# Weight sets moved to places of 1,056 columns, in a hybrid encoder layer on one Trainium2 core

## The chip, the core and the metric

The kernel runs on one core of one Trainium2 chip. A core has a matrix engine (TensorE; PE in the profile, its weight loads PEld), a vector engine (DVE), a scalar engine (ACT), GpSimd (POOL) and SyncE (SP), which here only issues transfers. They share an on-chip memory of 128 partitions. A TensorE instruction pair is a weight load of a 128x128 block and a matmul that streams up to 512 columns of a second operand, the moving one, through it. The metric is device microseconds of one execution. Three runs of the kernel before gave 1048.36, 1048.68 and 1045.71 us, the median is 1048.36.

## What is computed

One encoder layer over 512 positions of width 1024, in float32, with batch and depth of one. Modulation, norms, rotary embedding, a windowed and a differential attention and two gated feed-forward blocks:

```
mod = silu(c) @ w_mod + b_mod                      # nine vectors: shift, scale, gate three times
h = modulate(rmsnorm(x), sh1, sc1)
x = x + 0.5 * g1 * (silu(h @ w_gate1) * (h @ w_up1)) @ w_ffn1_out
h = modulate(rmsnorm(x), sh2, sc2)
qa, ka, va, qb, kb, vb, ga, gb = split(h @ w_in)
ya = window_gqa_sink(rope(norm(qa)), rope(norm(ka)), va) @ w_branch_a
yb = (rmsnorm(diff_attention(rope(norm(qb)), rope(norm(kb)), vb)) * 0.8) @ w_branch_b
x = x + g2 * ((sigmoid(ga) * ya + sigmoid(gb) * yb) @ w_out)
h = modulate(rmsnorm(x), sh3, sc3)
x = x + 0.5 * g3 * (silu(h @ w_gate3) * (h @ w_up3)) @ w_ffn2_out
```

The feed-forward width is 2816, so the two blocks hold most of the products.

## The kernel before

Every float32 operand of a product is split into a rounded part ("high") and the rest ("low"), and a product of blocks is three matmuls: high weights by high data, high by low, low by high. Line 173 (`mm3`) writes these three at lines 174 to 176. Line 437 (`two`) does the same for two blocks of 256 columns at lines 443 to 445; it serves the `Unit` class, which computes the feed-forward products by a seven-product scheme on quarter matrices. Lines 1125 to 1127 and 1144 to 1146 are projections in which the roles are changed: the weights' high and low parts are the moving operand and the hidden state is the stationary one. Line 681 is the first product of the kernel.

**Where weights lie.** A weight set of up to 1024 columns comes by DMA into a `raw` buffer, ACT rounds it into a set of the tile `high`, DVE writes the rest into the same columns of the tile `low` (`split_from`, line 189), or, in `load_main` (line 1059) and for three of the first sets, ACT and an accumulating DMA write the low part. Each of the two tiles has five places (HILO, line 98), taken in turn by `high_low` (line 197) unless a place is held. Places are 1024 columns apart, and a set may start some columns further on: the argument `aside`. The starts are ASIDE = 16 columns in every `Unit` (line 491), in the two later sets of line 923, in `project_pairs` (1136), in one gate (1165), in some sets of the last products of the first block (854), of a branch (1601) and of the mixing product (1663); FAR = 64 columns in the other sets of `Out1` (854); 8 or 56 in two steps from one rule to the next; 0 for the rest (first products, `project`, most gates, the other branch, six of the eight mixing sets). A set of 1024 columns that starts 16 columns aside ends in the first 16 columns of the next place. Dependencies are tracked by address, so there a write waits for the readers of the neighbour.

**Addresses.** Tiles are laid out in each partition in the order of their first use in the code, each rounded up to 32 bytes. Counting from the start of the pool at byte 4224: `high` begins at 22848 and `low` at 43584, both 64 bytes past a multiple of 256; the moving tiles `b8` (twelve of 8192 bytes from 68672) and `ka` also begin 64 past one, and the tiles `u4` (six of 4096 bytes from 167072) 160 past one. All slices of `b8` and `u4` that are used as operands start at multiples of 512 bytes in their tile. Blocks of weights are 128 columns, 512 bytes, apart. So the place of a weight block against its moving operand, taken modulo 256 bytes, is settled by the start of its set: 16 columns are 64 bytes, and 64 columns are 256. The text below calls (address of the weights minus address of the moving operand) modulo 256 bytes the **distance** of a matmul. It is 64 for the sets at 16 columns with `b8` as the moving operand, 0 for those at 0 and 64 columns, and 192 in the projection of line 1144, where the set (at 128) moves and `b8` (at 64) is stationary.

**What orders the work.** Most of the kernel is under a manual order for TensorE, DVE and ACT or for the queues: `run_items` (line 533) asks for each weight set some products ahead of its use and splits it some products ahead (ASK and MAKE, lines 459 and 460); a planner (`Line`, line 47) orders the attention.

Of the kernel before, what the change touches and what calls it, by code (L numbers as in the profile page):

```python
# [11 lines left out]
F32 = mybir.dt.float32  # L12
# [6 lines left out]
P = 128  # L19
# [77 lines left out]

RAW, HILO, F2 = 4, 5, 8

ASIDE = 16  # L100

FAR = 64


STEP, STEP_1 = 8, 56
BRANCH_ASIDES = (STEP, ASIDE, ASIDE, ASIDE), (ASIDE, ASIDE, 0, 0)
MIX_ASIDES = 0, 0, 0, 0, 0, 0, ASIDE, ASIDE

CHUNKS = (range(0, 6), range(6, 12), range(12, 16), range(16, 22))
PLAIN, LAST_1 = 3, 4  # L110
# [24 lines left out]
def layer(ctx: ExitStack, tc: tile.TileContext, a: dict):  # L135
# [58 lines left out]
    split = []  # L194
    turn, holders = [0], {}

    def high_low(n=1024, aside=0, holder=None):
        while turn[0] % HILO in holders:
            turn[0] += 1
        i = turn[0] % HILO  # L200
        turn[0] += 1
        if holder:
            holders[i] = holder
        i = i * 1024 + aside
        return tuple(t[:, i : i + n] for t in parts)

    def let_go(holder):
        for i in [i for i in holders if holders[i] == holder]:
            del holders[i]

    def load_split(src, n=1024, spare=False, aside=0):
        raw = sbuf("raw", [P, 1024], F32, RAW)
        if spare:
            hi, lo = (u4().rearrange("p a b -> p (a b)") for _ in range(2))
        else:
            hi, lo = high_low(aside=aside)
        nc.sync.dma_start(raw[:, 0:n], src)
        split_from(hi[:, 0:n], lo[:, 0:n], raw[:, 0:n])
        return hi, lo
# [4 lines left out]
    half = keep([P, 8], "half")  # L224
    V.memset(half, -0.5)
    S.activation(small(8), half, AF.Silu)
    ones = keep([P, P], "ones")
    V.memset(ones, 1.0)
    ident = keep([P, P], "ident")
    make_identity(nc, ident)  # L230

    par = keep([P, NPAR], "par")
    x = [xt() for _ in range(NC)]
    parts, modv = [], []
    for nm, n in (("high", 6), ("low", 9)):
        parts.append(keep([P, HILO * 1024 + ASIDE], nm, F32R))
        modv += [keep([P, NC], f"mod{v}") for v in range(len(modv), n)]
    sub8, lam_s, nlam = (keep([P, n], nm) for nm, n in (("sub8", 1), ("lam_s", 2), ("nlam", 1)))

    def mod_load(v, c, w=None):  # L240
        if w is None:
# [42 lines left out]
    class Norm:  # L284
# [41 lines left out]
        def sums(self, sq, r, first, last):  # L326
            if first:
                self.st[r.start] = bank("op" if r.start else "tp")
            for t in range(r.start // P, r.stop // P):
                i = 2 * (t - r.start // P)  # L330
                PE.matmul(
                    self.st[r.start][:, i : i + 2], sq[:, t * P : (t + 1) * P], ones[:, 0:2],
                    start=first and i == 0, stop=last and (t + 1) * P == r.stop, skip_group_check=True,
                )

# [111 lines left out]
    class Unit:  # L447
# [33 lines left out]
        def prepare(self, q):  # L481

            if q in self.ready:
                return
            self.ask(q)
            n = self.depth * 2 * P
            if q in self.apart:
                both = b8().rearrange("p a b -> p (a b)")
                hi, lo = both[:, 0:n], both[:, 1024 : 1024 + n]
            else:  # L490
                hi, lo = high_low(n, ASIDE, (self, q))
            t = self.at[q]
# [108 lines left out]

    cact = [sbuf("ka", [P, D], F32, 1)]
    hh, hl = new_h()
    ccol = keep([P, 3 * NC], "ccol")[:, 0:NC]
    nc.scalar.dma_start(ccol, a["c"])
    tc.keep_in_program_order(nc.scalar.dma_start(par, a["par"]))
    for c in range(NC):
# [2 lines left out]
    with tc.manual_schedule(engines=BOUND | {mybir.EngineType.SP, mybir.EngineType.Pool}):  # L610
# [14 lines left out]
                start=j == 0, stop=j == 3, skip_group_check=True,  # L625
            )
        warm(3)
        w1, pos = {}, []

        def first_loads(k):  # L630
            scale = mod_load(SC1, k)
            if k == 0:
                pos.append(keep([P, NT], "pos", I32))
            shift = mod_load(SH1, k) if k == 0 else None
            raw = sbuf("raw", [P, 1024], F32, RAW)
            nc.sync.dma_start(raw, a["w1s"][k])
            w1[k] = [scale, shift or mod_load(SH1, k), raw]
# [137 lines left out]
    pos = pos[0]  # L775
# [57 lines left out]
    class Out1:  # L833
# [14 lines left out]
        def by_halves(self, m):  # L848
            return self.final and m >= NC - LAST_1

        def prepare(self, m):
            if m not in self.ready:
                self.ask(m)
                aside = FAR if not self.by_halves(m) else STEP_1 if m == NC - LAST_1 else ASIDE
                if self.final and m == 0:
                    while turn[0] % HILO != 1:
                        turn[0] += 1
                t = self.ready[m] = high_low(self.depth * P, aside, (self, m))
                with tc.issue_after(copied[0]):
                    split_from(*t, self.at[m])  # L860

# [51 lines left out]
    with tc.manual_schedule(engines={mybir.EngineType.SP, mybir.EngineType.Pool}):  # L913
# [4 lines left out]
        for q in range(4, 2 * PLAIN):  # L918

            w, sums_from = loaded1, split[1]  # L920
            if q < 5:
                with tc.issue_after(split[0]), tc.issue_after(split[1]):
                    loaded1 = [load_split(a["w1i"][1, k], aside=ASIDE) for k in range(2)]
# [12 lines left out]
            if q == 4:  # L936
                units1[PLAIN].prepare("s1")
            side1(1.0)
# [44 lines left out]
    V.tensor_scalar(sub8, par[:, SUBLN : SUBLN + 1], 1.0 - LAM_INIT, None, ALU.mult)  # L983

    NF = HD // 2
    posf = keep([P, NT], "posf")
    V.tensor_copy(posf, pos)
    tb = u4(F32)
    tb = [tb[:, i, :] for i in range(2)]
# [66 lines left out]

    hh, hl = new_h()

    def load_main(src, aside=0):

        raw = sbuf("raw", [P, 1024], F32, RAW)
        nc.sync.dma_start(raw, src)
        hi, lo = high_low(aside=aside)
# [67 lines left out]
    def project_pairs(srcs, then):  # L1131

        n = 2 * P
        out = [bank("acc") for _ in range(2)]
        for u, src in enumerate(srcs):
            wh, wl = load_main(src, ASIDE)
            for t in range(NT):
                ht = slice(t * P, (t + 1) * P)
                po = out[t // 2][:, t % 2 * n : (t % 2 + 1) * n]
                for i in range(4):  # L1140
                    k = 4 * u + i
                    w = slice(i * n, (i + 1) * n)
                    first, last = k == 0 and t % 2 == 0, k == NC - 1 and t % 2 == 1
                    PE.matmul(po, hh[k][:, ht], wh[:, w], start=first, stop=False, skip_group_check=True)
                    PE.matmul(po, hh[k][:, ht], wl[:, w], start=False, stop=False, skip_group_check=True)
# [14 lines left out]
    def gates(more=lambda: True):  # L1160
        while gate_next[0] < 16 and more():
            j = gate_next[0]
            gate_next[0] += 1

            wh, wl = load_main(a["w_gate"][j], ASIDE * (j == EARLY_A))
# [77 lines left out]

    kb_h, kb_l, vb_h, vb_l, qb_h, qb_l = (b8() for _ in range(6))
    rqb = keep([P, NT, 8], "rqb")
    nrqb = keep([P, NT, 8], "nrqb")
    ob_h, ob_l = b8(), b8()
    done, turns = {"a": 0, "b": 0}, {"a": 0, "b": 0, "o": 0, "w": (0, 0), "q": 0, "t": 0}

# [143 lines left out]
    def tables_a():  # L1393
# [1 line left out]
        nc.sync.dma_start(late, table_scr)  # L1395
        table["qa"], table["ka"] = (four(late)[i : i + 2] for i in (0, 2))
        ka = sbuf("ka", [P, 2, T], F32R, 1)
        wa.update(k=(ka[:, 0, :], ka[:, 1, :]), rq=keep([P, NT, 8], "rqa"))

    def two_blocks(raw, nh, tabs, i, rs, scale8):  # L1400

# [193 lines left out]
            turns["w"] = (b, g * nk + kc + 1)  # L1595


    def branch(w, j0, o_h, o_l, then, load, r=FULL[0], asides=(0, 0, 0, 0)):
        for u in range(4):
            with tc.issue_after(banded_last[0]):  # L1600
                wh, wl = load(w[u], aside=asides[u])
            for i in range(2):
                j = 2 * u + i
                g = f2()[:, r]
# [8 lines left out]
    def main():  # L1613
# [30 lines left out]

        for i, r in enumerate(HALVES):
            line.drain(lambda: done["a"] >= 2 * i + 2)
            yield from branch(a["w_ya"], 0, *wa["o"], then_b, load_split, r, BRANCH_ASIDES[i])

    mix = []
    line.run(main())  # L1650
# [9 lines left out]
    nc.sync.dma_start(cact[0], c_scr.partition_broadcast(P))  # L1660
    mod_begin(G3)
    for m in range(NC):
        w = load_split(a["w_mix"][m], aside=MIX_ASIDES[m])

        def products(po, r, w=w):
            wh, wl = w
# [367 lines left out]
```

## Time and profile before

| | |
|---|---|
| median of three runs | 1048.36 us |
| the profiled execution | 1044.11 us, span from first to last instruction 1042.3 us |
| granted TensorE clock | 0.999 of full |
| TensorE busy | 1034.8 us, 99% of the span, 7348 matmuls |
| weight loads busy | 953.2 us, 91% |
| DVE, ACT, POOL busy | 785.5 us, 575.6 us, 165.7 us |
| moved | 220.92 MB, mean 212 GB/s |
| chain of work that ended last | TensorE 93%, DVE 3%, ACT 3% |

Busy time of TensorE says little by itself here: matmuls overlap each other, and the profile models their ends. The time from the start of one to the start of the next is what adds up to the span. It can be read from the timeline, which lists each matmul with its start: the starts of the first matmul of a stretch and of the first one behind it, divided by the number between them. The mean duration of a group is the modelled one, and it rises with the same stalls.

### The profile page before, as it was taken

To read this page: it belongs to the slowest core of one execution; us is meant where nothing else is said; L and a number is where in the kernel's file an instruction comes from. 1 tells how busy PE (TensorE), PEld (TensorE's weight loads), DVE (VectorE), ACT (ScalarE), POOL (GpSimd) and SP (SyncE) were. 2 spreads that over 40 slices of the span, in tenths; PEclk is the share of its full clock that TensorE was granted. 3 is DMA by queue.
4 is the path that set the end of the run, shared out by engine and by line. 5 is a ranking of instruction groups with operands and counts; after the bars stand their busy time and mean duration, and the time that the engine had idled before them with its cause. 6 is when DMAs were issued, how large, how long until landed. Compare 5 with 4: busy or idle time off the path is not lost.

```text
span 1042.3 us, 18751 instructions
## 1 busy us (share of the span) xinstructions
PE 1034.8 (99%) x7348; PEld 953.2 (91%) x7348; DVE 785.5 (75%) x1436; ACT 575.6 (55%) x948; POOL 165.7 (16%) x190
## 2 busy tenths in 40 slices
PE   9999999999999999999999999999999999999998
PEld 6889899899998998899888888989999999999998
DVE  6886667567796679859772588976899777877867
ACT  6664335234454442667785855525867556655553
POOL 1101110110110100543333101001111111112110
PEclk9999999999999999999999999999999999999999
DMA  9977786966984459796646834974498998989874
GB/s 366 346 218 187 242 235 198 275 173 180 259 207 150 149 203 410 232 261 140 179 97 184 242 124 158 366 229 112 98 238 190 244 226 206 231 216 220 208 150 127
DMA packets 68793, 220.92 MB, mean 212 GB/s; under 512 B 8288, under 2 KB 10976, under 8 KB 68704
## 3 DMA queue, kind: packets, MB, share of 16 engines
q1 hardware_dynamic: 46224, 146.52, 38.7%
q0 software_dynamic: 19344, 68.70, 35.1%
q10 hardware_dynamic: 3136, 4.51, 1.2%
q8 instruction: 57, 0.93, 0.3%
q14 instruction: 32, 0.26, 0.1%
HBM read 209.46 MB, written 10.23 MB: 211 GB/s over the span
## 4 chain that ended last, share of the span: by engine, by line
PE 93%; DVE 3%; ACT 3%; issue 0%; DMA 0%; POOL 0%; DVEq 0%; ACTq 0%; POOLq 0%
PE acc L443 7%; PE acc L444 7%; PE acc L445 7%; PE sc L443 6%; PE sc L445 6%; PE sc L444 6%; PE sc L174 5%; PE sc L175 5%; PE sc L176 5%; PE acc L174 4%; PE acc L176 4%; PE acc L175 4%; PE acc L1125 2%; PE acc L1126 2%; PE acc L1127 2%; PE tp L1203 1%
## 5 line engine op out<-in xcount | busy, mean ns | idle before, releaser
L190 ACT CAST high<-raw 128x1024 fp32r<-128x1024 f32 (+2 forms) x160 | 155.9, 985 | 149.8 <-PE sc L175 37.7
L190 DVE TENSOR_TENSOR low<-raw,high 128x1024 fp32r<-128x1024 f32 (+2 forms) x160 | 181.3, 1141 | 49.4 <-ACT high L190 48.5
L443 PE MATMUL acc<-b,high 128*128 128x256 f32 x508 | 140.9, 277 | 0.0
L444 PE MATMUL acc<-b,high 128*128 128x256 f32 x508 | 140.7, 277 | 0.1
L445 PE MATMUL acc<-b,low 128*128 128x256 f32 x508 | 140.6, 277 | 0.0
L445 PE MATMUL sc<-b,low 128*128 128x256 f32 x500 | 138.5, 277 | 0.0
L443 PE MATMUL sc<-b,high 128*128 128x256 f32 x500 | 138.5, 277 | 0.0
L444 PE MATMUL sc<-b,high 128*128 128x256 f32 x500 | 138.4, 277 | 0.0
L190 DVE TENSOR_TENSOR low<-u,high 128x1024 fp32r<-128x1024 f32 (+1 forms) x73 | 87.5, 1200 | 21.8 <-ACT high L190 20.3
L190 ACT CAST high<-u 128x1024 fp32r<-128x1024 f32 (+1 forms) x73 | 75.4, 1036 | 49.1 <-PE sc L175 16.2
L174 PE MATMUL sc<-b,high 128*128 128x512 f32 (+1 forms) x272 | 97.5, 359 | 0.0
L175 PE MATMUL sc<-b,high 128*128 128x512 f32 (+1 forms) x272 | 97.3, 358 | 0.0
L176 PE MATMUL sc<-b,low 128*128 128x512 f32 (+1 forms) x272 | 97.1, 357 | 0.0
L444 PEld LDWEIGHTS acc<-b,high 128*128 128x128 f32 x508 | 95.5, 188 | 0.4 <-DVE b L1818 0.3
L443 PEld LDWEIGHTS acc<-b,high 128*128 128x128 f32 x508 | 95.5, 188 | 0.3 <-ACT f L520 0.2
L445 PEld LDWEIGHTS acc<-b,low 128*128 128x128 f32 x508 | 95.4, 188 | 0.0
L443 PEld LDWEIGHTS sc<-b,high 128*128 128x128 f32 x500 | 94.1, 188 | 0.2 <-ACT f L520 0.2
L445 PEld LDWEIGHTS sc<-b,low 128*128 128x128 f32 x500 | 93.9, 188 | 0.1
L444 PEld LDWEIGHTS sc<-b,high 128*128 128x128 f32 x500 | 93.9, 188 | 0.0
L174 PE MATMUL acc<-b,high 128*128 128x512 f32 (+1 forms) x240 | 89.4, 372 | 0.3 <-DVE u L190 0.3
L176 PE MATMUL acc<-b,low 128*128 128x512 f32 (+1 forms) x240 | 87.1, 363 | 0.0
L175 PE MATMUL acc<-b,high 128*128 128x512 f32 (+1 forms) x240 | 86.9, 362 | 0.0
(387 smaller groups left out, 2713.5 us busy)
## 6 DMA issues: line engine op xcount, KB each, us to landing
u<-w_mod SPq DMA_DIRECT2D x40, 512.0 KB, 8.0
b<-w_mod SPq DMA_DIRECT2D x32, 512.0 KB, 5.7
raw<-w2i SPq DMA_DIRECT2D x31, 512.0 KB, 5.3
u<-w2i POOLq DMA_DIRECT2D x31, 512.0 KB, 7.1
u<-w1u POOLq DMA_DIRECT2D x24, 512.0 KB, 7.4
raw<-w1u SPq DMA_DIRECT2D x24, 512.0 KB, 6.7
raw<-w1o SPq DMA_DIRECT2D x24, 384.0 KB, 4.3
raw<-w_gate SPq DMA_DIRECT2D x16, 512.0 KB, 4.2
```

What stands on the lines that cost most here:

```text
L174: PE.matmul(out, wh, xh, start=first, stop=False)
L175: PE.matmul(out, wh, xl, start=False, stop=False)
L176: PE.matmul(out, wl, xh, start=False, stop=last)
L190: last = S.copy(hi, src), V.tensor_tensor(lo, src, f(hi), ALU.subtract)
L443: PE.matmul(out, wh[:, s], xh, start=first and j == 0, stop=False, skip_group_check=True)
L444: PE.matmul(out, wh[:, s], xl, start=False, stop=False, skip_group_check=True)
L445: PE.matmul(out, wl[:, s], xh, start=False, stop=last and j == 1, skip_group_check=True)
L1125: PE.matmul(out[t][:, 0:n], hh[k][:, ht], wh[:, o : o + n], start=k == 0, stop=False)
L1126: PE.matmul(out[t][:, 0:n], hh[k][:, ht], wl[:, o : o + n], start=False, stop=False)
L1127: PE.matmul(out[t][:, 0:n], hl[k][:, ht], wh[:, o : o + n], start=False, stop=k == NC - 1)
L1203: PE.transpose(tp[:, j * P : (j + 1) * P], src, ident)
```

## The change

Places become 1056 columns apart (4224 bytes, which is 128 more than a multiple of 256), and every set starts at the beginning of its place; all the asides go. So that the larger tiles fit, other tiles shrink, move, or share a buffer.

```diff
-ASIDE = 16
-FAR = 64
-STEP, STEP_1 = 8, 56
-BRANCH_ASIDES = (STEP, ASIDE, ASIDE, ASIDE), (ASIDE, ASIDE, 0, 0)
-MIX_ASIDES = 0, 0, 0, 0, 0, 0, ASIDE, ASIDE
+PLACE = 1024 + 32
...
-    def high_low(n=1024, aside=0, holder=None):
+    def high_low(n=1024, holder=None):
...
-        i = i * 1024 + aside
+        i = i * PLACE
         return tuple(t[:, i : i + n] for t in parts)
...
-    ones = keep([P, P], "ones")
+    ones = keep([P, 2], "ones")
...
+    sub8, lam_s, nlam = (keep([P, n], nm) for nm, n in (("sub8", 1), ("lam_s", 2), ("nlam", 1)))
+    pos = keep([P, 4 * NT], "pos", I32)[:, 0:NT]
+    parts, modv = [], []
+    def mods(n):
+        modv.extend(keep([P, NC], f"mod{v}") for v in range(len(modv), n))
+    mods(2)
     x = [xt() for _ in range(NC)]
-    parts, modv = [], []
-    for nm, n in (("high", 6), ("low", 9)):
-        parts.append(keep([P, HILO * 1024 + ASIDE], nm, F32R))
-        modv += [keep([P, NC], f"mod{v}") for v in range(len(modv), n)]
-    sub8, lam_s, nlam = (keep([P, n], nm) for nm, n in (("sub8", 1), ("lam_s", 2), ("nlam", 1)))
+    ccol = keep([P, 2 * NC], "ccol")[:, 0:NC]
+    for nm, n in (("high", 5), ("low", 6)):
+        parts.append(keep([P, HILO * PLACE - 24], nm, F32R))
+        mods(n)
...
-                hi, lo = high_low(n, ASIDE, (self, q))
+                hi, lo = high_low(n, (self, q))
...
-    ccol = keep([P, 3 * NC], "ccol")[:, 0:NC]
+    mods(9)
...
-                aside = FAR if not self.by_halves(m) else STEP_1 if m == NC - LAST_1 else ASIDE
...
-                t = self.ready[m] = high_low(self.depth * P, aside, (self, m))
+                t = self.ready[m] = high_low(self.depth * P, (self, m))
...
-    nrqb = keep([P, NT, 8], "nrqb")
+    nrqb = sbuf("freq", [P, NT, 8], F32, 1)
...
-        wa.update(k=(ka[:, 0, :], ka[:, 1, :]), rq=keep([P, NT, 8], "rqa"))
+        wa.update(k=(ka[:, 0, :], ka[:, 1, :]), rq=sbuf("Ckb", [P, NT, HD], F32, 1)[:, :, 0:8])
```

The rest of the diff takes `aside` out of the calls of lines 923, 1136, 1165, 1601, 1647 and 1663 and out of `load_split`, `load_main` and `branch`, and makes the tile `posf` early (line 633) where `pos` was made.

Counted in the same way, the new layout puts `high` at byte 22656, 128 past a multiple of 256, and `low` at 43776, a multiple of 256. `b8`, `ka`, `u4`, `raw`, `f2` and `x` keep their places modulo 256 (64, 64, 160, 192, 192 and 64). A set in place 0, 2 or 4 has its high part at 128 and its low part at 0; a set in place 1 or 3 has its high part at 0 and its low part at 128.

More of the change, by code (lines that the diff above doesn't have):

```diff
@@ L209, in let_go, with load_split @@
             del holders[i]
-    def load_split(src, n=1024, spare=False, aside=0):
+    def load_split(src, n=1024, spare=False):
         raw = sbuf("raw", [P, 1024], F32, RAW)
@@ L215, in load_split @@
         else:
-            hi, lo = high_low(aside=aside)
+            hi, lo = high_low()
         nc.sync.dma_start(raw[:, 0:n], src)
@@ L331, in sums @@
                 PE.matmul(
-                    self.st[r.start][:, i : i + 2], sq[:, t * P : (t + 1) * P], ones[:, 0:2],
+                    self.st[r.start][:, i : i + 2], sq[:, t * P : (t + 1) * P], ones,
                     start=first and i == 0, stop=last and (t + 1) * P == r.stop, skip_group_check=True,
@@ L627, in layer @@
         warm(3)
-        w1, pos = {}, []
+        w1, kept = {}, []
         def first_loads(k):
@@ L632, in first_loads @@
             if k == 0:
-                pos.append(keep([P, NT], "pos", I32))
+                kept.append(keep([P, NT], "posf"))
             shift = mod_load(SH1, k) if k == 0 else None
@@ L774, in layer @@
     row = u4(F32).rearrange("p a b -> p (a b)")[:, 0:NROW]
-    pos = pos[0]
     freq = keep([P, HD // 2], "freq")
@@ L846, in ask @@
                 nc.sync.dma_start(t, a["w1o"][m][:, c : c + n])
-        def by_halves(self, m):
-            return self.final and m >= NC - LAST_1
         def prepare(self, m):
@@ L922, in layer @@
                 with tc.issue_after(split[0]), tc.issue_after(split[1]):
-                    loaded1 = [load_split(a["w1i"][1, k], aside=ASIDE) for k in range(2)]
+                    loaded1 = [load_split(a["w1i"][1, k]) for k in range(2)]
             behind = split[1]
@@ L985, in layer @@
     NF = HD // 2
-    posf = keep([P, NT], "posf")
+    posf = kept[0]
     V.tensor_copy(posf, pos)
@@ L1057, in layer, with load_main @@
     hh, hl = new_h()
-    def load_main(src, aside=0):
+    def load_main(src):
         raw = sbuf("raw", [P, 1024], F32, RAW)
         nc.sync.dma_start(raw, src)
-        hi, lo = high_low(aside=aside)
+        hi, lo = high_low()
         S.copy(hi, raw)
@@ L1135, in project_pairs @@
         for u, src in enumerate(srcs):
-            wh, wl = load_main(src, ASIDE)
+            wh, wl = load_main(src)
             for t in range(NT):
@@ L1163, in gates @@
             gate_next[0] += 1
-            wh, wl = load_main(a["w_gate"][j], ASIDE * (j == EARLY_A))
+            wh, wl = load_main(a["w_gate"][j])
             out = bank("acc")
@@ L1595, in window_out, with branch @@
             turns["w"] = (b, g * nk + kc + 1)
-    def branch(w, j0, o_h, o_l, then, load, r=FULL[0], asides=(0, 0, 0, 0)):
+    def branch(w, j0, o_h, o_l, then, load, r=FULL[0]):
         for u in range(4):
             with tc.issue_after(banded_last[0]):
-                wh, wl = load(w[u], aside=asides[u])
+                wh, wl = load(w[u])
             for i in range(2):
@@ L1646, in main @@
             line.drain(lambda: done["a"] >= 2 * i + 2)
-            yield from branch(a["w_ya"], 0, *wa["o"], then_b, load_split, r, BRANCH_ASIDES[i])
+            yield from branch(a["w_ya"], 0, *wa["o"], then_b, load_split, r)
     mix = []
@@ L1662, in layer @@
     for m in range(NC):
-        w = load_split(a["w_mix"][m], aside=MIX_ASIDES[m])
+        w = load_split(a["w_mix"][m])
         def products(po, r, w=w):
```

## The prediction

> **What bounds the kernel now.** I read the page's busy shares and its chain first, then the waits of TensorE, then the timeline of stretches that differ only in where their weight sets start.
>
> ```profile
> span 1042.3 us, 18751 instructions
> ...
> PE 1034.8 (99%) x7348; PEld 953.2 (91%) x7348; DVE 785.5 (75%) x1436; ACT 575.6 (55%) x948; POOL 165.7 (16%) x190
> ...
> PEclk9999999999999999999999999999999999999999
> ...
> PE 93%; DVE 3%; ACT 3%; issue 0%; DMA 0%; POOL 0%; DVEq 0%; ACTq 0%; POOLq 0%
> ```
>
> TensorE works 99% of the span at the full granted clock, and 93% of the chain is its own. The waits of TensorE that the profile can name:
>
> ```profile
> PE acc L617 <- POOL ident masks.py:199: 1.3, 1, 1.3
> PE acc L681 <- ACT b L669: 0.4, 2, 0.2
> PE op L331 <- ACT f L292: 0.3, 1, 0.3
> PE acc L174 <- DVE u L190: 0.3, 1, 0.3
> ```
>
> They come to 2.3 us, three of the four lie in the start or in a norm, and none is a wait for a weight set in `high` or `low`. So waits that overlapping sets cause end, if anywhere, on ACT, DVE or POOL ahead of TensorE's need. What moves the time is the pace of 7348 matmuls: 1 ns on each is 7.3 us.
>
> The pace is not one number. In the timeline I take the first matmul of a stretch and the first one behind it (the columns are start, modelled duration, line, operands):
>
> ```profile
> 806.71 0.28 PE L443 MATMUL acc<-b,high 128*128 128x256 f32 x1
> ...
> 831.19 0.28 PE L443 MATMUL acc<-b,high 128*128 128x256 f32 x1
> ...
> 655.49 0.28 PE L174 MATMUL acc<-b,high 128*128 128x256 f32 x1
> ...
> 665.39 0.28 PE L174 MATMUL acc<-b,high 128*128 128x256 f32 x1
> ...
> 671.15 0.40 PE L174 MATMUL sc<-b,high 128*128 128x512 f32 x1
> ...
> 455.71 0.28 PE L1144 MATMUL acc<-high,b 128*128 128x256 f32 x1
> ...
> 461.37 0.28 PE L1144 MATMUL acc<-high,b 128*128 128x256 f32 x1
> ```
>
> Matmuls of 256 columns. The first pair encloses nine sets of 24, all 16 columns aside, distance 64: 24.48 us / 216 = 113.3 ns. The second encloses seven blocks of 12, also 16 aside and distance 64: 9.90 / 84 = 117.9 ns. From 665.39 to 671.15 follow 48 of the same line whose sets start at 0, distance 0: 5.76 / 48 = 120.0 ns. The last pair is two sets of the projection, distance 192: 5.66 / 48 = 117.9 ns. The same work at one clock takes 113.3, 117.9 or 120.0 ns, by the place of its weights; at distance 64 it has two paces.
>
> ```profile
> 676.62 0.39 PE L174 MATMUL sc<-b,high 128*128 128x512 f32 x1
> ...
> 703.81 0.28 PE L174 MATMUL sc<-b,high 128*128 128x256 f32 x1
> ...
> 71.36 0.40 PE L174 MATMUL acc<-b,high 128*128 128x512 f32 x1
> ...
> 82.56 0.28 PE L443 MATMUL sc<-u,high 128*128 128x256 f32 x1
> ```
>
> Matmuls of 512 columns: five sets at 0, distance 0, 27.19 us / 120 = 226.6 ns; two sets at 16, distance 64, 11.20 / 48 = 233.3 ns. Here the order is turned round: 64 is the slow distance.
>
> How many stand where? The widths and counts are in the groups by form:
>
> ```profile
> L443 PE MATMUL acc<-b,high 128*128 128x256 f32 x508 | 140.9, 277 | 0.0
> L443 PE MATMUL sc<-b,high 128*128 128x256 f32 x500 | 138.5, 277 | 0.0
> ...
> L443 PE MATMUL op<-b,high 128*128 128x256 f32 x94 | 26.0, 277 | 0.0
> ...
> L174 PE MATMUL sc<-b,high 128*128 128x512 f32 x192 | 74.8, 390 | 0.0
> ...
> L174 PE MATMUL acc<-b,high 128*128 128x512 f32 x176 | 71.3, 405 | 0.3 <-DVE u L190 0.3
> ...
> L681 PE MATMUL acc<-b,high 128*128 128x512 f32 x45 | 17.7, 392 | 0.2 <-ACT b L669 0.2
> ...
> L1125 PE MATMUL acc<-high,b 128*128 128x512 f32 x72 | 28.3, 393 | 0.0
> ...
> L1144 PE MATMUL acc<-high,b 128*128 128x256 f32 x96 | 27.8, 290 | 0.0
> ```
>
> Distance 64, 256 columns: the units (508, 500, 94, 94 and 16 with `ka`, three lines each, 3636) and 324 of lines 174 to 176, in all 3960. Their modelled mean of 277 ns stands between two others, taken inside the stretches above:
>
> ```profile
> L443 PE MATMUL acc<-b,high 128*128 128x256 f32 x60 | 16.6, 276 | 0.0
> ...
> L174 PE MATMUL acc<-b,high 128*128 128x256 f32 x28 | 7.9, 281 | 0.0
> ```
>
> 276 at the pace of 113.3, 281 at 117.9. So about four fifths have the good pace, and the mean is near 113.3 + 0.2 x 4.6 = 114.2 ns. Distance 0, 512 columns: 368 x 3 of line 174's family less 72 at 16 aside, 186 of line 681, 96 x 3 of line 1125's: 1506, at 226.7 to 227. Line 1144's family is 288 at distance 192.
>
> **The change part by part.** *No instruction is added or removed* in the products; operations, widths, orders and transfers stay. What is left is where things lie and what waits for what.
>
> *The asides go, 256 columns.* In the new layout the distance is 64 for the high part of a set in an even place and 192 for its low part; in an odd place the reverse. So the 3960 matmuls, now all at 64, become half 64 and half 192, mixed inside each group of three. 64 has 114.2 ns as a mean, 192 has only the row of 117.9, with the roles of the operands changed. Bounds of the mixture: all at the best row, 113.3 (-0.9 x 3960 = -3.6 us), or all at the worst, 120.0 (+5.8 x 3960 = +23.0 us). I take each matmul at the row of its own distance, (114.2 + 117.9) / 2 = 116.05 ns: +1.85 x 3960 = **+7.3 us**. It might be more, since the good pace would have to survive an interruption in every group of three.
>
> *The asides go, 512 columns.* The 1506 matmuls at distance 0 become half 64, half 192. For 64 there is the row of 233.3. For 192 with 512 columns there is none. Its bounds: at the low end 220.0, which is 226.7 less the 6.7 that separate the best and the worst row of 256 columns; at the high end 240.0, as far above 233.3. I take 230.0, the middle of the two rows of 512 columns, which it is as near to as can be said. Mean 231.65, +4.95 x 1506 = **+7.5 us**; with both halves at 220.0 it is -10.1 us, with 240.0 throughout +20.
>
> *The remaining matmuls.* The 288 of line 1144 go from 192 to a mixture of 192 and 64: -1.85 x 288 = -0.5 us. The units with a moving `u4` (160 past a multiple) go from a distance of 224 to 224 and 96:
>
> ```profile
> 853.04 0.28 PE L443 MATMUL sc<-u,high 128*128 128x256 f32 x1
> ...
> 855.84 0.28 PE L443 MATMUL sc<-b,high 128*128 128x256 f32 x1
> ```
>
> 2.80 / 24 = 116.7 ns for 224; 96 lies between 113.3 and 120.0, so within -3.4 and +3.3 ns for half of 456: below 0.8 us either way, taken as 0.
>
> *Overlap ends.* A write of a set no longer waits for the readers of its neighbour's last 16 columns. What could be gained on TensorE is inside the 2.3 us of waits above, and none of these is on a set: taken as -0.3 us, bounds 0 and -0.7 (the two waits at lines 681 and 174). ACT and DVE are at 55% and 75%; a set split earlier only waits longer for its use.
>
> *Shared buffers.* `nrqb` takes over the buffer of `freq`, `rqa` that of `Ckb`. Both are written by DVE, and the last readers of the old contents are DVE operations of an earlier stage, so DVE's own order covers the wait; if that cover failed, one wait of some 1 us would stand ahead of the scores, hidden in part. `ones`, `pos`, `posf`, the `mod` tiles and `ccol` only move. Nothing is queued anew on SP or POOL.
>
> Sum: 7.3 + 7.5 - 0.5 + 0 - 0.3 = +14.0 us. On the profiled execution, 1044.1 us with what lies around its span, that is 1058.1. That execution stood 4.3 us (0.4%) below the median of 1048.36, and a median is forecast: 1048.4 + 14.0, rounded to **1062**.
>
> **The rivals.**
>
> *(a) Alternation relieves TensorE: faster.* The stall of one matmul might come from its own phase against the next weight load, and a load half a period away might find the memory free. Place: every group of three. Price: 256 columns at 113.3 throughout (-3.6) and 512 at 220.0 (-10.1): 1048.4 - 13.7 - 0.3 = 1034; with only the 256 columns relieved, 1044. For it: at distance 64 there are two paces, so the phase matters beside the address, and a mixture could settle in the better one. Against: no row of 512 columns beats distance 0, and the only row at 192 has the slower pace. It decides where 3960 (a - 114.2) + 1506 (b - 226.7) falls below zero, with a and b the new means in ns.
>
> *(b) The memory repeats every 128 bytes.* Then 192 is as good as 64: 256 columns stay at 114.2, 512 columns all go to 233.3: +6.6 x 1506 = +9.9, less 0.3: 1058. For it: 117.9 is a pace of both distances. Against: the projection, interrupted many times, never shows 113.3; its mean is 279 and 280 in that stretch.
>
> ```profile
> L1145 PE MATMUL acc<-low,b 128*128 128x256 f32 x15 | 4.2, 279 | 0.0
> ...
> L1144 PE MATMUL acc<-high,b 128*128 128x256 f32 x14 | 3.9, 280 | 0.0
> ```
>
> *(c) The good pace is lost everywhere.* All 3960 at 117.9 (+14.7) and 512 columns at 233.3 (+9.9): 1073; at 120.0 and 240.0 up to 1091.
>
> *(d) Addresses don't matter, and the change does nothing but end the overlap.* Then only waits count: 1048.1. Against it stand five rows above, of equal shape and clock, that differ.
>
> Beside (d): the Trainium skill, in "TensorE: Matmul & The Clock Gate", section "Step-by-step: what each phase is for", gives TensorE two independent read ports, so that "loading the next tile's weights doesn't steal SBUF read bandwidth from the running matmul". By that rule no distance could cost anything and the time would stay at 1048. The trace differs: 113.3 against 120.0 ns at one clock, and the measurement decides here.
>
> **How the numbers follow.** Chances: the forecast, each distance at its own row, 0.36; (b) 0.18; (c) 0.14; (a) 0.25; (d) 0.07. The predicted time is the likeliest case's, 1062, whose own range is 1055 to 1069 (512 columns at 192 between 226.7 and 233.3 is 2.5 us either way, 256 columns a ns either way 4). The range for 8 in 10 takes in (b), most of (c) and the milder half of (a): 1040 to 1074. A measurement of this kernel can tell 0.3%, about 3 us, from no change (its three runs spread over 3 us). Slower by more: 0.36 + 0.18 + 0.14 = 0.68. Within: (d), 0.07. Faster: (a), 0.25.
>
> **What would show it right or wrong.** In the timeline of the new kernel: the stretch of units in the second feed-forward block should pace near 116 ns, with sets of even places better than those of odd ones; the mixing product's 512-column sets should pace above 227 ns. Modelled means of lines 443 to 445 should rise from 277 towards 279, of line 174's 512 columns from 390 towards 395. If the means fall to 276 and below 389, (a) holds and the forecast is wrong in its sign; if lines 443 to 445 stay and 512 columns rise to 396, (b). If neither moves, (d). TensorE's waits should stay under 3 us; a new wait for `high` or `low` would mean that I misread the places.

## The result, and the profile after

The changed kernel takes 1050.64 us, the median of 18 runs (1048.68 to 1054.17); the kernel before, run beside it, 1047.72 us (18 runs, 1044.83 to 1049.17). The ratio is 1.0036, 95% interval 1.0027 to 1.0046: slower by 0.36%, which is 3.8 us of 1048 (the two medians alone differ by 2.9). The forecast of 1062 had the sign, but it was 14 us where 3.8 were measured.

The page of the changed kernel shows the span, the busy times, the clock in 40 slices and the chain by engine. In the changed kernel lines 174, 1125 and 1144 are lines 167, 1120 and 1139; the experiments shift line numbers by a few, too.

```profile
span 1050.5 us, 18743 instructions
...
PE 1042.5 (99%) x7348; PEld 955.7 (91%) x7348; DVE 784.9 (75%) x1436; ACT 576.1 (55%) x948; POOL 165.1 (16%) x190
...
PEclk8999999999999999999999999999999999999999
...
PE 92%; ACT 3%; DVE 3%; DMA 1%; issue 1%; POOL 0%; ACTq 0%; DVEq 0%; POOLq 0%
```

The same matmuls, the same order, TensorE at 99%: what moved is again their pace. Its waits (engine, tile and line, what it waited for: us in total, times, longest):

```profile
PE sc L443 <- ACT f L520: 0.8, 1, 0.8
...
PE sc L445 <- DVE low L183: 0.3, 1, 0.3
PE acc L444 <- DVE b L1813: 0.2, 1, 0.2
```

These 1.3 us were not in the profile of the kernel before. The second is a wait for `low`, which the prediction had named as a sign of misread places; whether they belong to the change is taken up below (`buffers`). The timeline of the changed kernel, with the stretches that the prediction measured (first matmul of a stretch, first one behind it):

```profile
814.31 0.28 PE L443 MATMUL acc<-b,high 128*128 128x256 f32 x1
...
838.79 0.28 PE L443 MATMUL acc<-b,high 128*128 128x256 f32 x1
...
663.17 0.28 PE L167 MATMUL acc<-b,high 128*128 128x256 f32 x1
...
672.72 0.36 PE L167 MATMUL acc<-b,high 128*128 128x256 f32 x1
...
683.81 0.40 PE L167 MATMUL sc<-b,high 128*128 128x512 f32 x1
...
689.42 0.39 PE L167 MATMUL sc<-b,high 128*128 128x512 f32 x1
...
700.55 0.40 PE L167 MATMUL sc<-b,high 128*128 128x512 f32 x1
...
711.71 0.28 PE L167 MATMUL sc<-b,high 128*128 128x256 f32 x1
...
463.29 0.28 PE L1139 MATMUL acc<-high,b 128*128 128x256 f32 x1
...
468.93 0.28 PE L1139 MATMUL acc<-high,b 128*128 128x256 f32 x1
...
860.68 0.28 PE L443 MATMUL sc<-u,high 128*128 128x256 f32 x1
...
863.54 0.28 PE L443 MATMUL sc<-b,high 128*128 128x256 f32 x1
```

- Units of 256 columns: 24.48 us / 216 = 113.3 ns, as before. The three matmuls of a product now have the distances 64, 64, 192 in an even place and 192, 192, 64 in an odd one, and both kinds stand in this stretch.
- The blocks of line 167 with 256 columns: 9.55 / 84 = 113.7 ns, where it was 117.9. These became faster.
- 512 columns: the five sets from 683.81 to 711.71 take 27.90 / 120 = 232.5 ns, where it was 226.6. The first, in an odd place, 5.61 / 24 = 233.8; the next two, in even places, 11.13 / 48 = 231.9.
- The projection: 5.64 / 48 = 117.5 ns (117.9). The set whose moving operand is a `u4` tile: 2.86 / 24 = 119.2 ns (116.7).

The modelled means by form (same operands, same shape) say the same:

```profile
L443 PE MATMUL acc<-b,high 128*128 128x256 f32 x508 | 140.7, 277 | 0.0
...
L167 PE MATMUL sc<-b,high 128*128 128x512 f32 x192 | 75.6, 394 | 0.0
...
L1120 PE MATMUL acc<-high,b 128*128 128x512 f32 x72 | 28.6, 398 | 0.0
```

The 256 columns stayed at 277; the two groups of 512 columns went from 390 to 394 and from 393 to 398. Taken over all starts in the two traces (the time from a start to the next, with those longer than 1.25 of the median of their group left out as waits):

| matmuls | count | before, ns | after, ns | difference, us |
|---|---|---|---|---|
| 256 columns, moving `b8` or `ka` | 4080 | 114.26 | 113.77 | -2.0 |
| 256 columns, moving `u4` | 456 | 116.96 | 118.30 | +0.6 |
| 512 columns, weights in `high`/`low` | 1290 | 227.93 | 231.42 | +4.5 |
| 512 columns, projection (line 1120) | 288 | 227.17 | 230.70 | +1.0 |
| 256 columns, projection (line 1139) | 288 | 117.79 | 117.87 | 0.0 |
| 256 columns without `high`/`low` (two groups) | 384 | 119.37 | 118.80 | -0.2 |

The sum is +3.9 us, the size of the measured difference. The two profiled executions differ by 8.2 us (1052.27 and 1044.11), so 4.3 us of that lie elsewhere: about 2.5 in the start, the rest in waits. The same matmul of line 681 in the kernel before, then in the changed one, then in one of the experiments (`best`, below), which is faster than the kernel before:

```profile
20.02 0.39 PE L681 MATMUL acc<-b,high 128*128 128x512 f32 x1
```

```profile
23.01 0.40 PE L681 MATMUL acc<-b,high 128*128 128x512 f32 x1
```

```profile
22.99 0.39 PE L683 MATMUL acc<-b,high 128*128 128x512 f32 x1
```

The slice with clock 8 at the beginning of the page stands for this: in this execution the clock came up later, and 0.5 of the 3 us is made up again by 25 us. Of thirteen profiled kernels three began so, and one of them is faster than the kernel before; their mean granted clocks are 0.995 to 0.997. The kernel before varies likewise: of its 22 executions that were timed beside the first four experiments, the 12 with a mean granted clock below 0.9985 have a median of 1048.7 us, and the other 10 have 1046.2. So the change isn't needed for it.

### The profile page after: what moved, and what is told of

Read it like the earlier page. It is cut to its first block, busy times and chain, and to the rows that moved or that the text cites. A ratio compares the mean times of both kernels' runs of the same rounds, so it can differ in the third digit from the quotient of the medians.

```text
span 1050.5 us, 18743 instructions
## 1 busy us (share of the span) xinstructions
PE 1042.5 (99%) x7348; PEld 955.7 (91%) x7348; DVE 784.9 (75%) x1436; ACT 576.1 (55%) x948; POOL 165.1 (16%) x190
## 4 chain that ended last, share of the span: by engine, by line
PE 92%; ACT 3%; DVE 3%; DMA 1%; issue 1%; POOL 0%; ACTq 0%; DVEq 0%; POOLq 0%
PE acc L443 6%; PE acc L444 6%; PE acc L445 6%; PE sc L443 6%; PE sc L445 6%; PE sc L444 6%; PE sc L167 5%; PE sc L169 5%; PE sc L168 5%; PE acc L167 5%; PE acc L169 5%; PE acc L168 4%; PE acc L681 2%; PE sc L681 2%; PE acc L1120 2%; PE acc L1122 2%
```

## The experiments

All are edits of the kernel before. Where the two tiles need more room, `ones` is cut to half its columns and the small tiles are counted so that `b8`, `u4`, `high` and `low` keep their places modulo 256.

**Only the 256-column sets.** The low part of the sets 16 columns aside goes to 48 (72 matmuls of 512 columns and the projection of line 1144 are among them).

```diff
-        i = i * 1024 + aside
-        return tuple(t[:, i : i + n] for t in parts)
+        i = i * 1024
+        ah, al = (aside, 3 * ASIDE if aside == ASIDE else aside)
+        return tuple(t[:, i + a : i + a + n] for t, a in zip(parts, (ah, al)))
```

> The kernel before, with only the sets that stood 16 columns aside changed: their high part stays at 16 columns, their low part goes to 48. So in the 256-column products two matmuls of each three keep distance 64 and the third goes to 192, as in an even place of the changed kernel; sets at 0 and the 512-column products stay. Theory now (the mixture keeps the good pace): 3960 matmuls from a mean of 114.1 ns to 113.7-113.8, -1.4 us, with the 72 matmuls of 512 columns at 16 aside -0.1: ratio about 0.9985, lines 443 to 445 paced 113.3 to 113.7 in the timeline. My term on record (each distance at its own row, 192 at 117.9): a third of 3960 by 3.8 ns, +5.0 us, ratio 1.005. Rival (overlaps and waits make the difference, not the distance): 1.000 within 0.001.

Measured: 1046.58 us, ratio 0.9986 (0.9974 to 0.9998), a gain of 1.5 us where my term on record asks for a loss of 5. In its timeline:

```profile
657.05 0.28 PE L174 MATMUL acc<-b,high 128*128 128x256 f32 x1
...
666.58 0.36 PE L174 MATMUL acc<-b,high 128*128 128x256 f32 x1
...
807.51 0.28 PE L445 MATMUL acc<-b,high 128*128 128x256 f32 x1
...
831.99 0.28 PE L445 MATMUL acc<-b,high 128*128 128x256 f32 x1
```

9.53 / 84 = 113.5 ns, which was 117.9, and 24.48 / 216 = 113.3, which was 113.3. With every third matmul at 192 the stretch that had the slow pace has the good one, and the one that had the good pace keeps it. Over all starts the 4080 have 113.6 ns, where they had 114.26.

**Only the 512-column sets.** The same line, with `(ASIDE, 3 * ASIDE) if aside in (0, FAR) else (aside, aside)`: all sets that stood at distance 0.

> The kernel before, with only the sets that stood at distance 0 changed (at 0 or 64 columns): high part to 16 columns, low part to 48, so that the 512-column products and the 512-column projection go from distance 0 to 64, 64, 192 as in an even place; the 256-column sets at 16 stay. Theory now (leaving distance 0 is the loss): 1218 matmuls of line 174's and line 681's kind from 227.6 to 231.7 ns, +5.0 us, 288 of line 1125's kind from 227.2 to about 230.8, +1.0 us, some 60 of 256 columns that leave distance 0, -0.3 us: +5.7 us, ratio 1.0054. Rival (overlaps, waits and shared buffers make the loss of the change): 1.000. Rival (memory repeats every 128 bytes): all 1506 at 233.3, +8.9 us, ratio 1.0085.

Measured: 1065.32 us, ratio 1.0165 (1.0148 to 1.0181). Neither the theory nor a rival had that. The pace gives 5 to 6 us of it (start to start the 1290 have 231.97 ns, 4.0 more than before, +5.2; the projection's 288 have 230.4, +0.9). The rest is waiting, of this kernel's own making: a set at 16 columns behind one whose low part starts at 48 overlaps it by 32, in a place where the kernel before has no overlap. The waits of ACT, in the kernel before and then here:

```profile
ACT low L1065 <- PE acc L1145: 4.3, 3, 2.1
```

```profile
ACT low L1067 <- PE acc L1147: 19.4, 3, 12.8
```

ACT can't write the next low part before TensorE has read the last columns of the one ahead: 12.8 us, and the accumulating DMA behind it comes late. The next line is one window of this kernel: its length, the busy time (with the instructions) of PE, PEld, DVE, ACT and POOL, the granted clock, the share of DMA and its GB/s. TensorE stands still for 4.3 of 20 us, and the clock falls to 0.83, which in the kernel before is 1.00 in the same window:

```profile
460.00:480.00 20.00, 15.71 (x93) 13.70 (x93) 5.13 (x13) 5.63 (x8) 5.55 (x5) 0.83 0.66 160
```

The longest wait of TensorE there, 2.64 us for a DMA into `low`, ends at 472.88 us. For the next 6 us the granted clock is 0.50 to 0.54, and 25 matmuls from 473.26 to 478.59 us start every 213 ns, where those behind them start every 118: some 2.4 us more on top of the wait. So this run shows what an overlap costs where it comes at the wrong place, and not what the 512 columns cost by themselves. `both`, below, is for that.

**All sets 16 columns aside.** `i = i * 1024 + ASIDE`, whatever the argument.

> The kernel before, with every set 16 columns aside, high and low alike: no overlaps, one distance of 64 for all weights that are loaded, nothing alternates, buffers as before. Theory now: 1218 matmuls of 512 columns from 227.6 to the row of 233.3, +6.9 us; the 288 of the 512-column projection come to distance 192, 230 to 233 ns, +0.8 to +1.7 us; 256 columns that leave distance 0, -0.4 us: +7.3 to +8.2 us, ratio about 1.0075, which is more than the changed kernel's loss, since there a part of each three is eased by alternation. Rival (the loss of the change comes from waits, not from distances): 1.000. Rival (the end of the overlaps is a gain that the change's distances hide): clearly below 1.0075, by the waits of 2.3 us at most, 1.005.

Measured: 1051.48 us, ratio 1.0042 (1.0027 to 1.0057), less than the 1.0075 expected. The pace is as expected; five sets of 512 columns, the ones quoted of the kernel before:

```profile
684.68 0.39 PE L174 MATMUL sc<-b,high 128*128 128x512 f32 x1
...
712.68 0.28 PE L174 MATMUL sc<-b,high 128*128 128x256 f32 x1
```

28.00 / 120 = 233.3 ns. Over all its starts 512 columns cost +6.9 us (1290 x 5.36), the projection's 288 +0.5 (229.05 ns), and 256 columns give back 1.1 (113.99 against 114.26): +6.3 us, where the interval of the ratio ends at +6.0. The rival that the loss comes from waits (1.000) falls. Whether the end of all overlaps gives something back can't be told from this.

**A table of distances, 512 columns.** The sets of `Out1` at chosen places:

```diff
-                t = self.ready[m] = high_low(self.depth * P, aside, (self, m))
+                h, l = (64 + v // 4 for v in TABLE[self.chunks.start][m])
+                t = self.ready[m] = high_low(self.depth * P, (h, l), (self, m))
```

> The kernel before, with the sets of the down projection of the first feed-forward block at chosen distances, to read paces in one profile: its first chunk (6 sub-blocks) has its eight sets, all 512 columns, at distances 0, 32, ... 224, high and low alike; its third chunk the same in reverse order; its second chunk has pairs (high, low) of (64,192), (192,64), (0,128), (128,0), (0,64), (64,0), (0,192), (192,0); its last has 512 columns at (0,32), (32,0), (32,32), (0,0) and 256 columns at 128, 192, 32 and 96. Expected paces of 512 columns: 227 at 0, 233.3 at 64, for 64 with 192 231.5. If the memory repeats every 128 bytes: 227 at 128, 233.3 at 192; if the distance works within 256 bytes: 192 clearly other than 233.3. 256 columns: 117.9 at 192 by my row on record, 113.3 to 114 if 192 is as good as 64. If distances don't matter, all 512-column sets pace alike within 0.5 ns.

The starts of its first chunk. Sets of 18 matmuls stand at distance 0 from 110.20, 32 from 114.32, 64 and 96 from 118.51, 128 from 126.91, 160 from 131.09, 192 from 135.30, 224 from 139.43:

```profile
110.20 0.40 PE L180 MATMUL sc<-b,high 128*128 128x512 f32 x1
...
114.32 0.39 PE L180 MATMUL sc<-b,high 128*128 128x512 f32 x1
...
118.51 0.40 PE L180 MATMUL sc<-b,high 128*128 128x512 f32 x1
...
126.91 0.39 PE L180 MATMUL sc<-b,high 128*128 128x512 f32 x1
...
131.09 0.39 PE L180 MATMUL sc<-b,high 128*128 128x512 f32 x1
...
135.30 0.40 PE L180 MATMUL sc<-b,high 128*128 128x512 f32 x1
...
139.43 0.40 PE L180 MATMUL sc<-b,high 128*128 128x512 f32 x1
```

At 0: 4.12 / 18 = 228.9 ns, which in the kernel before is 226.7 in all sets of this chunk but the first; at 32: 232.8; at 64 and 96: 8.40 / 36 = 233.3; at 128: 232.2; at 160: 233.9; at 192: 229.4. In the third chunk, in reverse order, 192 had 233.8 and 128 had 232.6. So for 512 columns 0 is good, the other distances cost 5.5 to 7.2 ns, and 192 has two paces, of which the better costs 2.7. Distance 128 isn't like 0, so the pace doesn't repeat every 128 bytes, which was the reason of my rival (b). Of the pairs of high and low, each measured in one set of 18, (64,192) had 231.9, (192,64) 233.1, (0,64) 230.8 and (0,128) 231.7: the best, (192,0), had 229.2. No mixture reaches 226.7.

**Both, and no overlap.** All sets with high at 16 and low at 48.

> The kernel before with every set at one pair of places: high part 16 columns aside, low part 48, so all products have distances 64, 64, 192 as in an even place of the changed kernel, and no set overlaps its neighbour; buffers as before. It takes the waits of the run with only the 512-column sets away and leaves its paces. Theory now: 1218 matmuls of 512 columns from 227.6 to 232.0, +5.3 us; 288 of the 512-column projection from 227.2 to 230.4, +0.9; 256 columns -1.7; the weights that meet a moving tile of the kind u4 (a third of them at 96) +1.0: +5.5 us, ratio 1.005, and no wait for a set. Rival (my sum on record, each distance at its own row): +5.0 more for 256 columns, 1.011. Rival (overlap and shared buffers make the loss of the change): 1.000.

Measured: 1051.50 us, ratio 1.0035 (1.0021 to 1.0050): the same as the changed kernel, whose places, shared buffers and moved tiles it doesn't have. So the loss is the distances'. The five sets of 512 columns quoted of the other kernels:

```profile
684.54 0.39 PE L174 MATMUL sc<-b,high 128*128 128x512 f32 x1
...
712.36 0.28 PE L174 MATMUL sc<-b,high 128*128 128x256 f32 x1
```

27.82 / 120 = 231.8 ns, which was 226.6. Against the kernel with only the 256-column sets (0.9986) the 512 columns cost 0.0049, 5.1 us (by the two intervals, give or take 2).

**Only the shared buffers.** `nrqb = sbuf("freq", ...)` and `rq=sbuf("Ckb", ...)`, as in the change.

> The kernel before with the change's shared buffers alone: nrqb in the buffer of freq, rqa in that of Ckb; no address of a weight set changes. Theory now and on record: no difference, 1.000 within 0.001. Rival (the shared buffers bring a wait ahead of the scores): 1.001 or more, with a wait in the stretch from 460 to 560 us that the kernel before doesn't have. As all distances are those of before, its profile also shows whether the waits at 171 and 247 us, which every profile but that of before has, come without any change of distance: theory yes, they are there in some executions of any of these kernels.

Measured: 1047.02 us, ratio 1.0000 (0.9986 to 1.0015). In its waits:

```profile
PE sc L445 <- DVE low L190: 0.7, 1, 0.7
...
PE sc L443 <- ACT f L520: 0.2, 1, 0.2
```

Two of the waits that were new in the changed kernel's profile are here too, with every weight address as before; `all16`, with the buffers as before, has both as well. So neither the new addresses nor the shared buffers are needed for them; the one profile of the kernel before is without them. Ahead of the scores there is one new wait of 0.2 us, for `ka`, and `u192`, which doesn't share the buffers, has it too.

**The 256-column sets, with `u4` moved.** The first edit, and `u4` moved by 160 bytes (`ccol` has 64 columns instead of 24), so that 456 matmuls more come to 64, 64, 192. The change itself doesn't move `u4` in this way; its shared buffers are taken over to make room.

> The kernel with the 256-column sets at 16 (high) and 48 (low), as tried before (ratio 0.9986), and with the u4 tiles moved by 160 bytes to 64 past a multiple of 256, so that the 456 matmuls with a moving u4 come to distances 64, 64, 192 too; 512-column sets stay at distance 0. The shared buffers of the change make room for it. Theory now: 256 columns -1.4 us, the 456 from 117.0 to 113.5, -1.6 us, 240 others of 256 columns at another distance from 119.7 to between 113.5 and 120, -1.5 to +0.1: -3 to -4.5 us against before, ratio 0.997. Rival (117 is set by u4 being written or read otherwise, not by its distance): as the kernel without the move, 0.9986.

Measured: 1044.65 us, ratio 0.9979 (0.9967 to 0.9992), the fastest of the study. The set with a moving `u4` that took 116.7 ns before and 119.2 in the changed kernel:

```profile
854.33 0.28 PE L445 MATMUL sc<-u,high 128*128 128x256 f32 x1
...
857.04 0.28 PE L445 MATMUL sc<-b,high 128*128 128x256 f32 x1
```

2.71 / 24 = 112.9 ns. Over all starts the 456 have 113.5 ns, where the first edit alone left them at 118.8. Their weights start at the same places in both, and only the moving tile has moved: so for 256 columns the address of the weights by itself doesn't set the pace, and the distance, which takes in both operands, describes it. The expected 0.997 lies at the edge of the interval, and by the ratios alone this kernel can't be told from the first edit (0.9986).

**All sets at 0.** `i = i * 1024`.

> The kernel before with every set at the beginning of its place and places as before: distance 0 for all weights that are loaded. By the row of 120.0 ns: 3960 matmuls of 256 columns from 114.1 to 119.9, +22.8 us; the 288 of the 256-column projection from 117.8 to about 120, +0.6; 72 of 512 columns from 233.3 to 227, -0.4; the 456 with a moving u4, now at 160, between 113.3 and 120, -1.6 to +1.4: span about 1042 to 1044 plus 23, 1065 to 1068. If distances don't matter: 1044 to 1049.

One execution: 1067.71 us, span 1065.9, with the kernel before at 1046.75 beside it. The 4080 matmuls of 256 columns have 119.93 ns from start to start.

**A uniform 192.** What failed in my term, the row or its use? The sets 16 columns aside go to 48, high and low.

```diff
-        i = i * 1024 + aside
+        i = i * 1024 + (3 * ASIDE if aside == ASIDE else aside)
```

> The kernel before with its 256-column sets 48 columns aside instead of 16, high and low alike: the 3960 matmuls stay uniform, at distance 192 instead of 64. It tells what failed in my term for 256 columns. If the row of 117.9 ns holds for 192 and only its use in a mixture was wrong: 3960 x (117.8 - 114.1), +14.6 us, with +1.1 for the moving u4 tiles at 96: +15.5 us, ratio 1.015, a uniform 192 far worse than the mixture of 64 and 192 (0.9986). If 192 is simply as good as 64 (the row was the wrong one, the memory repeating every 128 bytes): +1 us, 1.001.

Measured: 1057.64 us, ratio 1.0110 (1.0092 to 1.0128), on the side of the first theory. The stretch of units:

```profile
814.05 0.28 PE L443 MATMUL acc<-b,high 128*128 128x256 f32 x1
...
839.49 0.28 PE L443 MATMUL acc<-b,high 128*128 128x256 f32 x1
```

25.44 / 216 = 117.8 ns. The row of 117.9 was right for 192; two matmuls at 64 with one at 192 are better on average than either alone. That the ratio stayed under 1.015 is partly the 456 with `u4`, which had 117.5 ns at 96, 0.5 more than before, where I had put +1.1 us (2.4 ns each), and the projection's 288, whose distance became 64 and which had 115.2 instead of 117.8.

**A table of pairs, 256 columns.** `high_low(n, tuple(v // 4 for v in PAIRS[self.nth % len(PAIRS)]), (self, q))`. Sets of neighbouring units write into up to 48 columns of each other, so the values of these products are others; the matmuls are the same.

> The kernel before, with each unit's sets at a pair (high, low) of distances, the pairs going round from unit to unit: (64,64), (64,192), (192,192), (192,64), (128 or 64 with the other), (64,0), (0,64), (64,96), (0,128), (128,128), to read paces of 256 columns; sets of neighbouring units may overlap and wait, so its time says nothing. Expected: (64,64) 113.3 or 117.8, (192,192) 117.8, (64,192) and (192,64) 113.3 to 114, (128,128) 119 to 120. If any pair half a period apart eases, (0,128) has 113 to 115; if each matmul has its distance's row, (0,128) has 119.7, (64,0) 115 to 119, and (64,192) 115.4.

Stretches without interruption, for the pairs (0,128), (64,192) and (192,64) in this order:

```profile
769.04 0.28 PE L445 MATMUL sc<-b,high 128*128 128x256 f32 x1
...
774.76 0.28 PE L445 MATMUL acc<-b,high 128*128 128x256 f32 x1
...
819.19 0.28 PE L445 MATMUL acc<-b,high 128*128 128x256 f32 x1
...
827.35 0.28 PE L445 MATMUL acc<-b,high 128*128 128x256 f32 x1
...
905.86 0.28 PE L445 MATMUL acc<-b,high 128*128 128x256 f32 x1
...
908.71 0.28 PE L445 MATMUL acc<-b,high 128*128 128x256 f32 x1
```

5.72 / 48 = 119.2; 8.16 / 72 = 113.3; 2.85 / 24 = 118.8 ns. A stretch of (0,64), from 1018.68 to 1032.82 us, has 14.14 / 120 = 117.8 ns. That high and low stand 128 bytes apart isn't enough, since (0,128) gains nothing; and (192,64), an odd place of the changed kernel, mostly has 118 to 119 here, where in the changed kernel it mostly has 113.3.

**Only the odd order.** High at 48, low at 16.

> The kernel before with the sets that stood 16 columns aside at 48 (high) and 16 (low): the 3960 matmuls of 256 columns have distances 192, 192, 64 throughout, the order of an odd place of the changed kernel, with no set of the even order between them. Theory now (a stretch keeps the pace it has come into; in the changed kernel the odd sets are carried by the even ones ahead of them): as in the table of pairs, where (192, 64) had 118.5 in 16 of 18 sets: 3960 x (118.5 - 114.1), +17 us, ratio 1.016. Rival (a mixture of 64 and 192 has the good pace in either order): 113.4 to 114, -0.5 to -2.8 us, 0.997 to 1.000.

Measured: 1053.57 us, ratio 1.0076 (1.0053 to 1.0098), between the two. The timeline shows why:

```profile
809.87 0.28 PE L444 MATMUL acc<-b,high 128*128 128x256 f32 x1
...
834.35 0.28 PE L444 MATMUL acc<-b,high 128*128 128x256 f32 x1
...
998.76 0.28 PE L444 MATMUL acc<-b,high 128*128 128x256 f32 x1
...
1010.18 0.28 PE L444 MATMUL acc<-b,high 128*128 128x256 f32 x1
```

24.48 / 216 = 113.3 ns in nine sets on end, and 11.42 / 96 = 119.0 in four others, at the same distances. A stretch has one of two paces and keeps it for many sets; in this trace it mostly changes at a set whose moving operand is `u4`. Theory and rival both had half of it: the odd order can carry the good pace, and it can't bring it about reliably. In the changed kernel, where even sets stand between them, 53 odd sets with a moving `b8` have about 113 ns and 6 have 119, and four of these six come right behind a set with a moving `u4`.

## Why the prediction was wrong

- *The pace bounds the kernel, waits do not.* Right: +3.9 us from the pace of six groups, against a ratio of 1.0036. That the sum had the right sign is partly luck: of its two large terms the first had the wrong sign.
- *256 columns, +7.3 us.* This step failed. It measured -2.0 in the changed kernel, and -1.5 us as a change by itself. The step was "I take each matmul at the row of its own distance". The row of 117.9 ns for 192 was right (uniform, 117.8 ns, ratio 1.011), and the price does not add by matmul: two of three at 64 and one at 192 have 113.3 ns, below the mean of their rows, and the sets of the reverse order between them mostly have it too. The bound of the good row, -3.6 us, was in the prediction; I took the middle with no row of a mixture to support it, and gave the relief of rival (a) 0.25.
- *512 columns, +7.5 us.* Right in cause and sign, too large: +5.5 in the trace (4.5 and 1.0), 5.1 us between `both` and `only256`. The new mean, 231.65, was met (231.4 for weights in `high` and `low`, 230.7 in the projection). The old one was not 226.7 throughout: the 1218 at distance 0 had 227.6, since sets between other work pace slower. That the new mean was met is partly luck: 230.0 for 192 was the middle of two rows, and the table shows 229.4 and 233.8 there.
- *Line 1144, -0.5 us.* No change: 117.8 to 117.9 ns, though half of these changed their distance from 192 to 64.
- *Moving `u4`, 0.* +0.6 us.
- *End of the overlaps, -0.3 us; shared buffers, 0.* `buffers` is at 1.0000, and `both`, without overlaps, at the changed kernel's ratio. The overlaps of the kernel before cost nothing that was measured, which fits an order of asides that keeps them where the neighbour has been read; at the wrong place they come with some 11 us beyond the pace (`only512`, 17.3 less 6.1).
- *The rivals.* (a) described the 256 columns, down to its 113.3 ns, and failed for 512, where no mixture reached 226.7; its 1044 with only the 256 columns relieved had left out that 512 columns lose. (b) had nearly the pattern, 256 kept and 512 lost, by a reason that the tables refute: 128 isn't like 0, nor a uniform 192 like 64. (c) has its first half in the uniform 192, which the change doesn't make. (d) falls with `all0`, 21 us slower with nothing but the starts of the sets changed. The Trainium skill, "TensorE: Matmul & The Clock Gate", section "Step-by-step: what each phase is for", says that loading the next weights takes no read bandwidth from the running matmul, through a second, independent read port. The prediction's reading of it, that no distance could then cost anything, doesn't hold here; the runs don't show by what way the distance acts.

Shown: that the loss is the 512-column matmuls leaving distance 0, and that the 256 columns gain by the mixture. Open: why 512 columns want 0 and 256 columns 64 with 192, and what sets a stretch into one pace or the other. Open too, for 512 columns: in all runs their other operand stayed where it was, so their distance and the address of the weights by itself aren't told apart.

## What to carry to other kernels

When the pace of equal matmuls differs by stretch, put a pattern, not only single values, on the chip before adding up: costs per address were not additive here, and a mixture beat each of its parts. A change that helps one shape and hurts another should be split by shape: the half for 256 columns alone gave 0.9986 where the whole gave 1.0036 (and 0.9979 with `u4` moved as well). And compare the two profiles matmul by matmul before blaming a new wait: of 8.2 us between them, 4.3 lay in one execution's start and in waits, and a late start and two of these waits are there without the change as well.

## What was unexpected of the hardware

- The same 256-column products run at 113.3 or 119.0 ns for tens of microseconds with the same distances (`odd256`): a stretch keeps one of two paces; at a uniform 64 the two are 113.3 and 117.9.
- At a uniform distance of 0, 512 columns have their best pace (226.7 ns) and 256 columns one of their slowest (120.0).
- In `only512`, behind a wait of 2.64 us in a stretch with other gaps, the granted clock was 0.50 to 0.54 for 6 us, and matmuls of 118 ns took 213: the wait cost some 2.4 us more than its length.
